# Hybrid mLSTM and convolution block on one core: other places in memory for the operands of the 512-column products

## The chip, the cores and the metric

One Trainium2 chip, one of its cores. The metric is the device time of one execution in microseconds (us); a lower one is better. In the traces PE is TensorE's matmul, PEld its weight load, DVE is VectorE, ACT is ScalarE, POOL is GpSimd and SP is SyncE, whose queue issues the DMAs.

## What is computed

One layer over 2048 tokens of 1024 channels, in float32. After an RMS norm one projection makes the inputs of an mLSTM (four heads of 256) and of a convolution module; their two outputs are concatenated and projected back:

```python
u = rmsnorm(h, norm_g[l])
proj = jnp.einsum('bsd,de->bse', u, w_in[l])          # 1024 -> 8200 columns
...
hm = mlstm_chunkwise(q, k, v, i_pre, f_pre)            # then sigmoid(o), head norm, silu(z)
...
c = glu_a * jax.nn.sigmoid(glu_g)                      # then causal conv of width 31, layernorm, silu
...
mix = jnp.concatenate([hm, c.astype(x.dtype)], axis=-1)
h = h + jnp.einsum('bse,ed->bsd', mix, w_out[l])       # 2048 -> 1024 columns
return rmsnorm(h, final_norm_g)
```

## The kernel before

Each float32 operand of the two projections is split into two float32r tiles, a high part and the rest (hi and lo). A product of two such operands is three matmuls: hi times hi, hi times lo, lo times hi, summed in PSUM.

The tokens are worked on in two halves of 1024. For a half, the normed input lies in eight tiles `u` of 128 rows by 2048 columns, hi in the first 1024 and lo in the others. The weights stream through: SyncE loads a raw piece `wr` of two blocks of 512 columns, and for each block `w_prep_` (lines 209 to 223) makes one tile `w` of 1152 columns. ACT casts the block into hi (line 221), POOL subtracts it from the block and writes lo (line 222). Four such tiles are held, and they are made up to three ahead of their use (`WAHEAD`).

`unit` (line 311) is the product loop. It has three forms:

- `fm` (line 336), for the convolution's inputs, its gate, q and k: the weight is the stationary operand (128 of its columns) and the input is the moving one (512 tokens).
- `tm2` (line 343), for v, o and z of the heads: the input is stationary (128 tokens) and the weight is moving (256 columns).
- `tm` (line 350), for v of head 0 with the gates (264 columns), and for the output projection at the end (512 columns): the input or mix tile is stationary and the weight is moving.

Every matmul has a weight load of its own, of 128 by 128. Between the products of a unit a list of mLSTM steps and of convolution taps is worked off (`ml_slot`, `pump`), so that PE's stream of 512-column products is interrupted by small products (lines 601, 627, 631, 714), while DVE runs the convolution (line 787). The output projection (1536 products) comes last; in its second half nothing else runs on PE.

Where the operands lie: the third entry of a row of the list `wsrc` is the column at which hi begins in its `w` tile; lo begins 512 columns after it (for the 528-column blocks of the 264-column products: 0 and 576):

```python
odd = wsrc[i // 2][2]
...
both = wp.tile([P, 1152], F32R, tag="w", name=f"w{i}")
o2 = 576 if n == 528 else odd + 512
hi, lo = both[:, odd : odd + n], both[:, o2 : o2 + n]
```

In the program as built, all tiles `u`, `u_m` (the mix's) and `w` begin at a byte address in their partition that is 128 modulo 256. The pieces inside `u` and `u_m` lie at multiples of 512 bytes. So the place of a stationary operand past its moving one, modulo 256 bytes, is:

| products | count | moving columns | stationary past moving |
|---|---|---|---|
| `fm`, line 336 | 3840 | 512 | 0 |
| `tm` of the output, line 350 | 1536 | 512 | 0 |
| `tm2`, line 343 | 4224 | 256 | 64 |
| `tm` of head 0, line 350 | 384 | 264 | 0 and 224, half each |

The 64 of `tm2` comes from `ODD` = 48 columns, 192 bytes, by which the moving weight is shifted.

Of the kernel before, what the change touches and what calls it, by code (L numbers as in the profile page):

```python
# [39 lines left out]
def hybrid_block_kernel(  # L40
# [15 lines left out]
    WARM = 16  # L56


    PAD, ODD = 8, 48

    def pool(name, bufs, **kw):
        return ctx.enter_context(tc.tile_pool(name=name, bufs=bufs, **kw))
# [129 lines left out]
    wsrc = []  # L192
# [714 lines left out]
    WID = {}  # L907
# [13 lines left out]
    for hf in range(2):  # L921
        s = [("g", 0)]
        for h in range(NH):
            s += [("v", h)] + ([("g", 1)] if h == 0 else []) + [("o", h), ("z", h), ("q", h), ("k", h)]
            if h < 3:
                s += [("g", 2 * h + 2), ("g", 2 * h + 3)]
        s += [("c", j) for j in range(4)]
        seq.append(s)
        for u in s:
            if u == ("v", 0):  # L930
                for _ in range(2):
                    for g in range(2):
                        wsrc.append((wv0[g], 528, 0))
            else:
                for g in range(2):
                    wsrc.append((wu[WID[u], g], 512, ODD if u[0] in "ozv" else 0))
    for b in range(4):
        for nn in range(2):
            for g in range(8):
                wsrc.append((wo[nn, g], 512, 0))  # L940

    w_load(0)
    wstate["raw"] = 1
# [183 lines left out]
```

## Time and profile before

| | |
|---|---|
| time, median of 3 runs | 2008.14 us (2007.59 to 2011.28) |
| profiled execution | 2014.07 us, span 2012.4 us |
| mean granted TensorE clock | 0.993 of full speed |
| busy: PE, PEld | 98%, 87% of the span |
| busy: DVE, ACT, POOL | 72%, 41%, 39% |
| DMA | 204.10 MB, 30.6% of 16 engines' span |

The profiled execution is one of its own: it took 2014.07 us, of which 2012.4 lie between its first and its last instruction, and is 5.9 us (0.3%) above the median of the runs. A matmul's recorded duration contains its way through the pipeline and overlaps the next one's. What a matmul costs in a row of them is therefore read from starts: the start of the first to the start of what follows, divided by their number.

### The profile page before, as it was taken

What the parts mean: (1) busy time and instruction counts of PE and PEld (TensorE: products, weight loads), DVE (VectorE), ACT (ScalarE), POOL (GpSimd) and SP (SyncE); (2) the same over time, 40 slices, a digit from 0 to 9 for tenths busy, and PEclk for the clock granted to TensorE, in tenths of its full rate; (3) what the DMA queues carried; (4) which work ended last, traced back from release to release, by engine and by line L of the source; (5) the groups of instructions that cost most, each with busy time, mean ns of one, the idle gap of its engine ahead of it and who ended that gap; (6) DMA issues with size and microseconds to landing.
All of it is one profiled execution on the core that took longest, in us unless ns stands there. A gap on an engine that the chain in (4) does not pass through costs nothing.

```text
span 2012.4 us, 29602 instructions
## 1 busy us (share of the span) xinstructions
PE 1975.9 (98%) x11562; PEld 1744.7 (87%) x11562; DVE 1445.4 (72%) x1915; ACT 827.7 (41%) x1703; POOL 792.3 (39%) x740
## 2 busy tenths in 40 slices
PE   8999999999999999999999999999999999999998
PEld 7998998899899888888889879988998887788887
DVE  6598887699679765557799998977896658733221
ACT  5233432442343246545345224424523555543332
POOL 4632432333243332433333324333432236565564
PEclk9999999999999999999999999999999999999999
DMA  4121121212122233335211211211221566766452
GB/s 151 64 69 53 58 74 43 63 49 74 42 69 74 74 110 125 113 126 162 85 53 53 69 42 59 74 53 53 64 74 53 163 220 200 248 231 231 155 190 95
DMA packets 85836, 204.10 MB, mean 101 GB/s; under 512 B 7296, under 2 KB 40256, under 8 KB 85696
## 3 DMA queue, kind: packets, MB, share of 16 engines
q1 hardware_dynamic: 85696, 202.21, 30.6%
q8 instruction: 91, 1.49, 0.3%
q14 instruction: 49, 0.40, 0.1%
HBM read 159.15 MB, written 43.03 MB: 100 GB/s over the span
## 4 chain that ended last, share of the span: by engine, by line
PE 73%; DVE 18%; DMA 3%; issue 2%; ACT 2%; POOL 0%; SPq 0%; POOLq 0%; DVEq 0%; ACTq 0%
PE gm L336 32%; PE gm L343 18%; PE gm L350 16%; DVE y L787 11%; PE num L601 3%; PE kv L601 2%; PE sk L627 1%; DMA ly<-ysc 1%; DVE sm L302 1%; DMA wr<-in_wo 1%; PE mt L714 1%; DVE ly L844 1%; DMA ysc<-y 1%; PE sk L631 1%; ACT ly L881 0%
## 5 line engine op out<-in xcount | busy, mean ns | idle before, releaser
L222 POOL TENSOR_TENSOR w<-wr,w 128x512 fp32r<-128x512 f32 (+1 forms) x392 | 603.1, 1543 | 878.2 <-ACT w L221 859.4
L336 PE MATMUL gm<-u_u,w 128*128 128x512 f32 x3840 | 908.6, 392 | 0.7 <-DVE u_u L293 0.6
L336 PEld LDWEIGHTS gm<-u_u,w 128*128 128x128 f32 x3840 | 712.5, 188 | 143.2 <-DVE u_u L293 1.3
L787 DVE SCALAR_TENSOR_TENSOR y<-c,vec,y 128x1024 f32<-128x1024 f32 x480 | 714.5, 1489 | 9.7
L343 PE MATMUL gm<-w,u_u 128*128 128x256 f32 x4224 | 521.9, 281 | 5.7 <-DVE oz L451 3.4
L343 PEld LDWEIGHTS gm<-w,u_u 128*128 128x128 f32 x4224 | 505.8, 190 | 7.6 <-DVE oz L451 3.6
L221 ACT CAST w<-wr 128x512 fp32r<-128x512 f32 (+1 forms) x392 | 241.4, 620 | 591.6 <-PE gm L336 200.2
L350 PE MATMUL gm<-w,u_m 128*128 128x512 f32 x1536 | 355.0, 392 | 3.1 <-POOL w L222 1.9
L350 PEld LDWEIGHTS gm<-w,u_m 128*128 128x128 f32 x1536 | 289.1, 189 | 64.2 <-POOL w L222 2.8
L281 DVE TENSOR_TENSOR u_m<-mr,u_m 128x1024 fp32r<-128x1024 f32 x32 | 47.2, 1475 | 77.7 <-ACT u_m L280 77.7
L1019 DVE TENSOR_TENSOR ht<-gm,ht 128x512 f32<-128x512 f32 x32 | 21.5, 687 | 112.2 <-PE gm L350 112.2
L700 POOL TENSOR_TENSOR ss<-ss,nhalf 128x1 f32<-128x1 f32 x64 | 55.5, 867 | 111.9 <-ACT sq L699 111.3
L633 DVE SCALAR_TENSOR_TENSOR w<-sk,rs,ee 128x128 f32<-128x128 f32 x64 | 22.0, 344 | 81.6 <-PE sk L631 79.1
L601 PE MATMUL kv<-v,kw 128*128 128x258 f32 x360 | 74.3, 291 | 0.6 <-DVE cs L666 0.4
L666 DVE SCALAR_TENSOR_TENSOR cs<-cs,g_so,kv 128x258 f32<-128x258 f32 x112 | 53.3, 476 | 25.1 <-PE kv L601 24.7
L639 ACT ACTIVATE kw<-sk,g_wa 128x256 fp32r<-128x256 f32 x60 | 28.3, 472 | 81.7 <-DVE w L633 81.6
L719 ACT ACTIVATE mo<-mt,vec 128x128 f32<-128x128 f32 x128 | 39.7, 362 | 52.3 <-PE mt L714 52.1
L601 PEld LDWEIGHTS kv<-v,kw 128*128 128x128 f32 x360 | 56.9, 190 | 3.2 <-DVE cs L666 0.6
L408 DVE SCALAR_TENSOR_TENSOR v<-gm,rs,v 128x256 fp32r<-128x256 f32 x64 | 29.5, 475 | 33.4 <-ACT v L407 33.4
L699 ACT ACTIVATE sq<-hm 128x257 bf16<-128x257 f32 x64 | 26.9, 420 | 64.6 <-DVE hm L694 64.4
L761 POOL TENSOR_TENSOR c<-c,g 128x512 f32<-128x512 f32 x32 | 40.9, 1284 | 30.4 <-ACT g L760 27.6
L350 PE MATMUL gm<-w,u_u 128*128 128x264 f32 x384 | 50.8, 294 | 0.0
(200 smaller groups left out, 1818.0 us busy)
## 6 DMA issues: line engine op xcount, KB each, us to landing
wr<-in_wu SPq DMA_DIRECT2D x123, 512.0 KB, 3.6
wr<-in_wo SPq DMA_DIRECT2D x64, 512.0 KB, 3.6
mr<-mixs SPq DMA_DIRECT2D x32, 512.0 KB, 4.6
ysc<-y SPq DMA_DIRECT2D x16, 512.0 KB, 2.6
mixs<-mo SPq DMA_DIRECT2D x32, 256.0 KB, 2.1
zsc<-zc SPq DMA_DIRECT2D x32, 256.0 KB, 2.1
ly<-ysc SPq DMA_DIRECT2D x16, 512.0 KB, 5.2
lz<-zsc SPq DMA_DIRECT2D x16, 512.0 KB, 6.0
```

The source lines that it names most:

```text
L221: nc.scalar.copy(hi, s)
L222: nc.gpsimd.tensor_tensor(out=lo, in0=s, in1=hi.bitcast(F32), op=ALU.subtract)
L281: nc.vector.tensor_tensor(out=l_, in0=src, in1=h_.bitcast(F32), op=ALU.subtract)
L336: nc.tensor.matmul(ps[i], wt[:, o + cb * P : o + (cb + 1) * P], at[:, tb * 512 : (tb + 1) * 512], start=st, stop=sp_,)
L343: nc.tensor.matmul(ps[i][:, t2 * 256 : (t2 + 1) * 256], at[:, t * P : (t + 1) * P], wt[:, o : o + ncol], start=st and t2 == 0, stop=sp_, s ...
L350: nc.tensor.matmul(ps[i][:, :ncol], at[:, t * P : (t + 1) * P], wt[:, o : o + ncol], start=st, stop=sp_,)
L601: nc.tensor.matmul(ps, x_, y_, start=start and i == 0, stop=stop and i == 2)
L666: nc.vector.scalar_tensor_tensor(out=cs[:, d], in0=cs[:, d], scalar=so[:, h, c : c + 1], in1=kv[:, :VW], op0=ALU.mult, op1=ALU.add,)
L700: nc.gpsimd.tensor_tensor(out=ss, in0=ss, in1=nhalf[:, 0:1], op=ALU.pow)
L719: nc.scalar.activation(mo[:, d, (cc % 2) * P : (cc % 2 + 1) * P], mt[:, d * P : (d + 1) * P], AF.Identity, scale=col(V_MG, 2 * h + d),)
L761: nc.gpsimd.tensor_tensor(out=c[:, sl], in0=c[:, sl], in1=g, op=ALU.mult)
L787: tc.keep_in_program_order(nc.vector.scalar_tensor_tensor(out=y, in0=c[:, j + i * H2 : j + (i + 1) * H2], scalar=col(V_CW, b * CW + j), in1=y,
```

## The change

It alters the third entry of `wsrc` for the weights of the 512-column products, and nothing else. The `fm` weights (stationary) are shifted by 48 columns, 192 bytes, as the `tm2` weights (moving) already were. The output weights (moving) are shifted by 16 columns, 64 bytes. In the changed program as built, the stationary operand of all 5376 products of 512 columns begins 192 bytes past the moving one, modulo 256. The places of the other products are those of before, the order of the instructions on every engine too, and a `w` tile still has room: 48 + 512 + 512 = 1072 of its 1152 columns.

```diff
-    PAD, ODD = 8, 48
+    PAD, ODD, OUT = 8, 48, 16
...
                 for g in range(2):
-                    wsrc.append((wu[WID[u], g], 512, ODD if u[0] in "ozv" else 0))
+                    wsrc.append((wu[WID[u], g], 512, ODD))
     for b in range(4):
         for nn in range(2):
             for g in range(8):
-                wsrc.append((wo[nn, g], 512, 0))
+                wsrc.append((wo[nn, g], 512, OUT))
```

## Rows read from the trace of the kernel before

**Rows 1.** The page's part 1: busy time, share of the span, instructions of each engine

```profile
span 2012.4 us, 29602 instructions
...
PE 1975.9 (98%) x11562; PEld 1744.7 (87%) x11562; DVE 1445.4 (72%) x1915; ACT 827.7 (41%) x1703; POOL 792.3 (39%) x740
```

**Rows 2.** Groups by line, shapes apart: count, busy us, mean ns, idle us before

```profile
L336 PE MATMUL gm<-u_u,w 128*128 128x512 f32 x3840 | 908.6, 392 | 0.7 <-DVE u_u L293 0.6
...
L343 PE MATMUL gm<-w,u_u 128*128 128x256 f32 x4224 | 521.9, 281 | 5.7 <-DVE oz L451 3.4 <-ACT oz L438 1.7 <-DVE v L408 0.5
...
L350 PE MATMUL gm<-w,u_m 128*128 128x512 f32 x1536 | 355.0, 392 | 3.1 <-POOL w L222 1.9 <-DVE ht L1019 1.2
```

**Rows 3.** The chain that ended last, its last long piece: start us, us

```profile
1762.31 238.51 PE gm L350 x1052
```

**Rows 4.** PE's timeline, undisturbed 512-column products: start us, us, line, count

```profile
1824.75 179.46 PE L350 MATMUL gm<-w,u_m 128*128 128x512 f32 x791
```

**Rows 5.** The same, from 307 us, and the small products after it

```profile
307.75 48.45 PE L336 MATMUL gm<-u_u,w 128*128 128x512 f32 x213
356.04 0.60 PE L627 MATMUL sk<-q,k 128*128 128x128 f32 x4
356.48 0.38 PE L631 MATMUL sk<-ident,k 128*128 128x128 f32 x2
```

**Rows 6.** The same, two runs of 256-column products and what follows each

```profile
284.73 22.94 PE L343 MATMUL gm<-w,u_u 128*128 128x256 f32 x201
307.51 17.86 PE L336 MATMUL gm<-u_u,w 128*128 128x512 f32 x78
...
469.79 13.47 PE L343 MATMUL gm<-w,u_u 128*128 128x256 f32 x113
483.10 17.18 PE L336 MATMUL gm<-u_u,w 128*128 128x512 f32 x75
```

**Rows 7.** The same, a run of 264-column products and what follows it

```profile
851.78 7.18 PE L350 MATMUL gm<-w,u_u 128*128 128x264 f32 x58
858.80 17.88 PE L336 MATMUL gm<-u_u,w 128*128 128x512 f32 x78
```

**Rows 8.** The same, 512-column products just after small ones of the mLSTM

```profile
219.69 1.08 PE L336 MATMUL gm<-u_u,w 128*128 128x512 f32 x4
220.61 0.41 PE L601 MATMUL kv<-v,kw 128*128 128x258 f32 x2
...
221.79 1.32 PE L336 MATMUL gm<-u_u,w 128*128 128x512 f32 x5
222.95 0.28 PE L601 MATMUL num<-c0h,qssl 128*128 128x258 f32 x1
```

**Rows 9.** Stretches: us, busy us of each engine, granted clock, DMA share, GB/s

```profile
495.00:583.00 88.00, 88.00 (x441) 74.64 (x440) 61.96 (x87) 32.61 (x69) 33.13 (x31) 1.00 0.17 54
...
880.00:1045.00 165.00, 157.70 (x922) 138.51 (x920) 130.37 (x165) 78.03 (x148) 54.30 (x42) 0.98 0.34 110
1045.00:1240.00 195.00, 186.46 (x1169) 167.77 (x1169) 181.74 (x238) 77.68 (x174) 70.41 (x65) 0.97 0.18 56
...
1642.00:1820.00 178.00, 172.54 (x756) 140.80 (x755) 107.32 (x85) 85.59 (x151) 105.87 (x81) 0.99 0.70 236
1820.00:2004.00 184.00, 184.00 (x813) 152.49 (x812) 46.13 (x43) 63.06 (x114) 101.17 (x93) 1.00 0.48 163
```

**Rows 10.** Stretches, products of line 336 alone: PE and PEld busy us and count

```profile
880.00:1045.00 165.00, 92.96 (x391) 71.94 (x389) 0.98 0.34 110
1045.00:1240.00 195.00, 92.59 (x384) 72.95 (x384) 0.97 0.18 56
```

**Rows 11.** Line 221 from 286 us (weights at 192 bytes), from 310 us (at 0): min/median/max ns

```profile
L221 ACT CAST w<-wr x4: 620/624/664, 286.4 to 302.3; 128x512 fp32r<-128x512 f32 x4
...
L221 ACT CAST w<-wr x8: 621/622/638, 310.2 to 345.9; 128x512 fp32r<-128x512 f32 x8
```

**Rows 12.** Line 222 in the same two stretches: min/median/max ns

```profile
L222 POOL TENSOR_TENSOR w<-wr,w x4: 1290/1493/1562, 287.2 to 303.0; 128x512 fp32r<-128x512 f32 x4
...
L222 POOL TENSOR_TENSOR w<-wr,w x8: 1291/1296/2222, 310.9 to 346.6; 128x512 fp32r<-128x512 f32 x8
```

## The prediction

> **What bounds the kernel.** I read the busy shares first: PE is busy for 98% of the span, the next engine, DVE, for 72% [rows 1]. Then the groups by line: before all 5376 products of 512 columns PE sat idle for 3.8 us in sum (0.7 and 3.1), before the 256-column ones for 5.7 us [rows 2]. So PE is not waiting for data; it works through a list, and the time is the number of products by the spacing of their starts. The chain of waits says the same where it is plainest: its last long piece is 1052 products of line 350 in 238.51 us with nothing between them, 226.7 ns each [rows 3].
>
> A duration in a group's row (392 ns) is no price, since it overlaps the next product's. The price is the spacing, which the timeline gives:
>
> - 512 columns, output: 791 products in 179.46 us. Taking off the last one's own 0.39 us, 790 spacings take 179.07 us: **226.7 ns** [rows 4].
> - 512 columns, line 336: 213 products from 307.75 to the next line's start at 356.04, 48.29 us: again 226.7 ns [rows 5].
> - 256 columns, line 343: 201 products from 284.73 to 307.51, **113.3 ns**; in another stretch 113 products from 469.79 to 483.10, **117.8 ns** [rows 6].
> - 264 columns: 58 products from 851.78 to 858.80, 121.0 ns [rows 7].
>
> In stretches of this kind the granted clock is 1.00 [rows 9], the level of 2.4 GHz. A column per period would be 213.3, 106.7 and 110.0 ns for 512, 256 and 264 columns (an estimate from the clock alone). The rest is what each product pays beyond its columns: **13.3 ns** at 512 columns, **6.7 or 11.1 ns** at 256, **11.0 ns** at 264. Each product also comes with a load of 128 by 128 that PE does beside the stream; my reading is that the rest is this load getting in the way of the moving stream's reads.
>
> What differs between these rows is the width, and the place of the stationary operand against the moving one: 0 at 512 columns, 64 at 256, 0 and 224 by turns at 264. The smallest rest is at 64. But the 256-column products show two rests at one and the same place, so the place is not all of it: there are states that last over hundreds of products.
>
> **The change, part by part.**
>
> *It adds no work.* The instructions, their order, their sizes and their waits are those of before on every engine; SP's loads and POOL's and ACT's queue keep their turn, so nothing is moved past anything.
>
> *The writes of the weight tiles* move by 192 or 64 bytes. The trace has both places: ACT's cast takes 624 ns at 192 and 622 ns at 0 [rows 11], POOL's subtraction has a minimum of 1290 and 1291 ns [rows 12]; its medians, 1493 and 1296, rest on four and eight of them. Even 200 ns more on each of the 288 tiles that move (160 for line 336, 128 for the output) would be 58 us on an engine with 1220 us free of its 2012 [rows 1], working up to three tiles ahead of PE: nothing on the path. If that cover went, the two waits for POOL before line 350, now 1.9 us in all [rows 2], would grow first.
>
> *The reads of the 5376 products* are the only term: 3840 of line 336 and 1536 of line 350 [rows 2], each with a rest of 13.3 ns now. The trace has no 512-column product at the place 192, so the new rest is bounded:
>
> - Best case, 3.3 ns: four products of line 627 take 0.44 us, 110.0 ns each for 128 columns [rows 5]. That is 106.7 plus 3.3 ns at two periods a column: their stream asks for data half as fast, and beside it the load costs almost nothing. Gain 10.0 ns by 5376, 53.8 us: 1954 us.
> - Worst case, 18.7 ns: just after the mLSTM's small products, groups of four and five 512-column products run at 230 and 232 ns (219.69 to 220.61, 221.79 to 222.95) [rows 8]. These products pay more because something in the meeting of load and stream is out of its usual step. 232.0 less 226.7, 5.3 ns by 5376, is 28.5 us more: 2037 us.
>
> I take a value nearest to the only long rows with a place other than 0, those of the 256-column products: the mean of their two rests, 8.9 ns, 4.4 ns less than now. The two rests are also the ends of this case: 6.7 ns less gives 35.8 us, 2.2 ns less gives 11.8 us. The mean gives **23.7 us**. I carry the rest in ns over, not in proportion to the columns, because there is one load per product, whatever its width.
>
> *Where a saving would not arrive.* From 1045 to 1240 us DVE is busy 181.74 of 195 us and PE already stands for 8.5; from 880 to 1045 PE stands for 7.3, and from 1642 to 1820 for 5.5 [rows 9]. There another engine or a transfer is late next. The first two hold 775 products of line 336 [rows 10], the third at most 756 of line 350. At 4.4 ns that is 6.7 us of saving, of which I write off 2 us. Elsewhere DVE has room (61.96 of 88 us in a stretch of line 336, 46.13 of 184 at the end [rows 9]), and what a faster PE triggers, DMAs first, uses half the engines at the end.
>
> **The sum.** The profiled execution's 2014.1 us (span 2012.4) becomes 2014.1 - 23.7 + 2.0 = 1992.4. The median of the runs lies 5.9 us below that execution, so the same difference against the median of 2008.1 gives **1986.4 us**, 1.1% less.
>
> The Trainium skill speaks against it: "SBUF — State Buffer", section "SBUF: two separate sides", says that PE never waits on anyone at the memory's ports and names a second, independent read port for the weight loads. By that rule operands' places could not matter, and the sum would be 2008 us.
>
> The Trainium skill ("TensorE: Matmul & The Clock Gate", section "Wait — 56ns, not 53.3ns?") gives 215.7 ns for back-to-back products of 512 columns; an estimate from it would be 11.0 ns less on each, 59 us, 1949 us. The rows here show 226.7 and never less over a long stretch.
>
> **The rivals.**
>
> *The place does not matter* (12%). The load costs a fixed 13 ns or so, because the array has to take it in, whoever reads where. For it: the 264-column products pay 11.0 ns at places 0 and 224, the 256-column ones 11.1 ns in one of their states at 64: much the same. Against it: a fixed cost could not be 6.7 ns for 201 products on end and 13.3 ns right behind them [rows 5, 6]. Time 2008 us, within 4 us. (This is also the time by the skill's rule of the two ports.)
>
> *The place is a worse one* (21%). A stationary operand 192 past the moving one is as well 64 behind it, the mirror of the 256-column products' 64 ahead. A load that starts behind the stream it runs beside may run into it for longer than one that starts at the same place, and leave it out of step for good, as rows 8 show it for a few products. It decides if the lasting spacing exceeds 226.7 ns; at 232 ns the time is 2037 us. Against it: the 264-column products, half of them at 224, 32 behind, pay 11.0 ns on the whole and thus no more than others.
>
> *The load gets wholly out of the way* (9%). Then the rest falls towards the 3.3 ns of the best case, and the time to 1954 us, or a little above it, where DVE becomes the bound between 1045 and 1240 us.
>
> *The change misses its places.* If the tiles lay elsewhere than the text of the diff suggests, anything could come out. The addresses of the program as built exclude it: all 5376 products are at 192.
>
> **How the numbers follow.** My forecast, a rest between 6.7 and 11.1 ns, has 58%, and its own range is 1972 to 1996 us. With the larger gain, faster has 67%; no change has 12%, slower 21%. About 0.2%, 4 us, is what a measurement of this kernel can tell from no change. The range begins at the best case, 1954 us, below which I leave 4%. Upward it takes in no change and half the price of the worse place, 2022 us; beyond it I leave some 14%.
>
> **What would show it.** After the change the 791 products at the end should be spaced by 220 to 224.4 ns, and the 213 of line 336 alike; the 256-column products should keep 113.3 and 117.8, and line 221 and 222 their durations. PE's idle time between 1045 and 1240 us should grow by 1 or 2 us. A spacing of 226.7 in both would prove the first rival, one of 230 or more the second. The forecast would also be wrong, with a right spacing, if the 256-column products changed their states for the worse: all of them at 117.8 instead of 113.3 would cost up to 4.5 ns by 4224, 19 us. And if lines 336 and 350 came out apart, the place modulo 256 would not be what counts, since they share it.

## The result and the profile after

| | before | after |
|---|---|---|
| median of 6 runs | 2007.89 us (2004.48 to 2011.41) | 2019.57 us (2018.53 to 2021.27) |
| profiled execution, span | 2014.07 us, 2012.4 us | 2020.03 us, 2018.3 us |
| mean granted TensorE clock | 0.993 | 0.996 |

The change makes the kernel slower by 0.56%: the ratio is 1.0056, with a 95% interval of 1.0043 to 1.0069, 11.7 us on the medians. 1986.4 us had been forecast.

A line of the page's part 1, and the groups by line with the shapes apart, answer to [rows 1] and [rows 2]:

```profile
PE 1982.8 (98%) x11562; PEld 1739.7 (86%) x11562; DVE 1442.2 (71%) x1915; ACT 828.3 (41%) x1703; POOL 794.9 (39%) x740
```

```profile
L336 PE MATMUL gm<-u_u,w 128*128 128x512 f32 x3840 | 915.9, 394 | 0.2 <-DVE oz L451 0.2
L343 PE MATMUL gm<-w,u_u 128*128 128x256 f32 x4224 | 518.7, 280 | 6.0 <-DVE oz L451 3.4 <-ACT oz L438 1.6 <-DVE v L408 0.7
L350 PE MATMUL gm<-w,u_m 128*128 128x512 f32 x1536 | 359.1, 395 | 3.0 <-POOL w L222 1.8 <-DVE ht L1019 1.2
```

Nothing new waits. PE's busy time is 6.9 us longer: line 336 has 7.3 us more, line 350 has 4.1 us more, line 343 has 3.2 us less. The spacing of the undisturbed products tells why. PE's timeline (start us, us, line, count) at the end, then from 284 us, from 469 us, and from the first 512-column product after that:

```profile
1829.64 174.58 PE L350 MATMUL gm<-w,u_m 128*128 128x512 f32 x762
```

```profile
284.79 21.47 PE L343 MATMUL gm<-w,u_u 128*128 128x256 f32 x188
306.10 6.11 PE L336 MATMUL gm<-u_u,w 128*128 128x512 f32 x26
...
307.70 47.54 PE L336 MATMUL gm<-u_u,w 128*128 128x512 f32 x207
355.08 0.60 PE L627 MATMUL sk<-q,k 128*128 128x128 f32 x4
```

```profile
469.78 12.18 PE L343 MATMUL gm<-w,u_u 128*128 128x256 f32 x102
...
481.79 50.09 PE L336 MATMUL gm<-u_u,w 128*128 128x512 f32 x214
531.72 0.61 PE L627 MATMUL sk<-q,k 128*128 128x128 f32 x4
```

Worked out as before: the output's 762 products have (174.58 - 0.39) / 761 = **228.9 ns**, against 226.7 in [rows 4]. Line 336 has two spacings now where it had one: 47.38 us / 207 = **228.9 ns** from 307.70, against 226.7 in [rows 5], and 49.93 / 214 = **233.3 ns** from 481.79. The 256-column products are as they were, 113.4 and 117.7 ns in these two stretches, as in [rows 6]. The chain's last long piece (start us, us) answers to [rows 3], 228.9 ns a product:

```profile
1765.93 240.82 PE gm L350 x1052
```

Over the whole span, waits of more than 40 ns beyond the columns left out, the starts of line 336 are 230.4 ns apart on the mean (227.7 before) and those of the output 229.0 (227.0). 2.7 ns by 3840 and 2.0 ns by 1536 make 13.4 us; line 343 gives back 0.3 ns by 4224, 1.2 us. That leaves 12.2 us, against the 11.7 us of the medians. The two profiled executions themselves lie only 5.9 us apart: the one of before is 5.9 us above its median and has some 6 us more outside these spacings. From 880 to 1045 and from 1045 to 1240 us its granted clock was 0.98 and 0.97 [rows 9]; in the changed kernel's execution it was 0.99 and 1.00.

### The profile page after: what moved, and what is told of

Read it like the earlier page. It is cut to its first block, busy times and chain, and to the rows that moved or that the text cites. A ratio compares the mean times of both kernels' runs of the same rounds, so it can differ in the third digit from the quotient of the medians.

```text
span 2018.3 us, 29602 instructions
## 1 busy us (share of the span) xinstructions
PE 1982.8 (98%) x11562; PEld 1739.7 (86%) x11562; DVE 1442.2 (71%) x1915; ACT 828.3 (41%) x1703; POOL 794.9 (39%) x740
## 4 chain that ended last, share of the span: by engine, by line
PE 78%; DVE 15%; ACT 2%; issue 2%; DMA 2%; POOL 0%; SPq 0%; POOLq 0%; DVEq 0%; ACTq 0%
PE gm L336 35%; PE gm L343 18%; PE gm L350 17%; DVE y L787 9%; PE num L601 3%; PE kv L601 2%; PE sk L627 1%; DMA ly<-ysc 1%; PE mt L714 1%; DVE ly L844 1%; PE sk L631 1%; DMA ysc<-y 1%; DVE sm L302 0%; DVE y L777 0%; DVE qssl L592 0%
## 5 line engine op out<-in xcount | busy, mean ns | idle before, releaser
L350 PE MATMUL gm<-w,u_m 128*128 128x512 f32 x1536 | 359.1, 395 | 3.0 <-POOL w L222 1.8
```

Of the source, the lines that this page charges most:

```text
L350: nc.tensor.matmul(ps[i][:, :ncol], at[:, t * P : (t + 1) * P], wt[:, o : o + ncol], start=st, stop=sp_,)
```

## The experiments

All kernels below are the one before with other shifts. `place` gives the columns by which a unit's weight tile is shifted, `OUTS` the same for the output's; a shift by n columns puts line 336's stationary operand 4n bytes past the moving one, and lines 343's and 350's 4n bytes behind it. The edits are written short, against the kernel before. Below, "place" is the stationary operand's address less the moving one's, modulo 256 bytes. Spacings in tables are means over a stretch of products at one place, without waits of over 40 ns.

**Many places in one kernel.** `s1_places`, `s2_fine`, `s3_states` and `s4_rest` give a place of its own to each q and k unit (in `s3_states` all of them have 192), to each output unit and, from the second on, to the 256-column products of each head. The edit, here in the first:

```diff
+    FM1 = {(0, 0): (64, 128), (0, 1): (64, 128), (0, 2): (32, 96), (0, 3): (160, 224),
+           (1, 0): (16, 48), (1, 1): (64, 128), (1, 2): (32, 96), (1, 3): (160, 224)}
+    def place(hf, u):
+        nm, i = u
+        if nm in "ozv":
+            return 48
+        return (FM1[hf, i][nm == "k"] if nm in "qk" else 0) // 4
+    OUTS = {(0, 0): 48, (0, 1): 32, (1, 0): 0, (1, 1): 48, (2, 0): 32, (2, 1): 16, (3, 0): 56, (3, 1): 8}
...
-                    wsrc.append((wu[WID[u], g], 512, ODD if u[0] in "ozv" else 0))
+                    wsrc.append((wu[WID[u], g], 512, place(hf, u)))
...
-                wsrc.append((wo[nn, g], 512, 0))
+                wsrc.append((wo[nn, g], 512, OUTS[b, nn]))
```

> One kernel with several places. The stationary operand's place past the moving one, modulo 256 bytes, is for the eight output units in turn 64, 128, 0, 64, 128, 192, 32, 224; for the q and k units of heads 0 to 3 of the first half 64 and 128, 64 and 128, 32 and 96, 160 and 224; of the second half 16 and 48, 64 and 128, 32 and 96, 160 and 224; g and c units at 0 as before, the 256-column products at 64 as before. Theory A (each place modulo 256 has lasting spacings of its own): units at 0 again 226.7 ns, the unit at 192 again 228.9 or 233.3 ns, and at least one of 32, 64, 96 or 128 clearly under 226.7 (220 to 224.4 at 64). Theory B (equal places are best, every shift costs): all units but those at 0 at 228 to 234 ns. Theory C (the place is not what counts, but that a tile is shifted at all, or its writes): all shifted units alike, at 228.9 or 233.3, whatever the shift.

> A second kernel with several places. The 512-column products: small shifts around 0 (stationary past moving by 4, 8 and 12 bytes, or behind it by 4, 8 and 16), further places (80, 112, 144, 176, 208), and shifts by whole 256 and 512 bytes (place 0 again). The 256-column products of one head each: 0, 0, 128, 192 in the first half, 224, 96, 160, 32 in the second, in place of 64. Theory B1 (equal places modulo 256 are best, and only they): 226.7 ns at shifts of 256 and 512 bytes, 233.3 ns at most others, already at 16 bytes. Theory D (a tile that does not begin where it did is dearer, whatever the place): 228.9 ns or more at 256 and 512 bytes too. For the 256-column products, theory B1 carried over gives their least spacing at 0 (113.3 ns or less); if 64 was their best place, all others stand at 116 to 120 ns.

> A search for a better place, with those that have not been measured. 512 columns: 20, 28, 36, 40, 44, 52, 60, 68, 76, 84, 88, 92, 104, 108, 116, 120 in the q and k units, 132, 200, 152, 212, 164, 20, 148, 88 in the output units. 256 columns: 4, 24, 112, 144 in the heads of the first half, 12, 208, 240, 252 in those of the second. Theory B1 (0 is the one good place at 512 columns, 64 at 256): none under 226.7 ns at 512 columns, none under 115.9 ns on the mean at 256. If the spacings at 512 columns scatter between 2 and 4 pieces of 6.7 ns with no rule, one or two might fall to 220 ns, and all products could then take that place for some 30 us.

One run each took 2023.53, 2023.64 and 2024.69 us (before: 2009 to 2010). The spacings in ns, a choice of some fifty places measured at 512 columns:

| place, 512 columns | 0 | 4 | 8 | 16 | 20 | 32 | 60 | 64 | 96 | 120 |
|---|---|---|---|---|---|---|---|---|---|---|
| line 336 | 226.7 | 232.3 | 230.7 | 233.3 | 233.3 | 233.2 | 230.1 | 233.3 | 234.2 | 226.7 |
| line 350 | 226.7 | | 231.7 | | 228.9 | 233.3 | | 233.3 | | 233.5 |

| place, 512 columns | 128 | 148 | 160 | 176 | 192 | 208 | 224 | 236 | 240 | 252 |
|---|---|---|---|---|---|---|---|---|---|---|
| line 336 | 232.4 | | 233.3 | 230.0 | 228.9, 233.3 | 233.3 | 233.3 | | 228.3 | 233.4 |
| line 350 | 232.4 | 228.9 | | 231.1 | 228.9 | 233.3 | 233.3 | 239.7 | 231.6 | 237.9 |

| place, 256 columns | 0 | 16 | 32 | 56 | 60 | 64 | 68 | 72 | 96 | 128 | 144 | 160 | 192 | 224 | 252 |
|---|---|---|---|---|---|---|---|---|---|---|---|---|---|---|---|
| line 343, mean | 119.7 | 117.3 | 118.4 | 120.4 | 120.0 | 115.9 | 118.1 | 120.0 | 118.1 | 118.7 | 114.7 | 119.8 | 117.6 | 116.9 | 122.8 |

No place at 512 columns lies under 226.7 ns: 0 has the least, shared by 120 at line 336 alone. Theories C and D (any shift costs, whatever the place) fall: shifts of 256 and 512 bytes, place 0 again, give 226.7, and the others differ. Theory A's forecast that 64 is good at 512 columns falls. At 256 columns the order is another one: 0 is among the worst, 64 and 144 are the best, and 4 bytes beside 64 the products stand at 118 to 120. PE's timeline of `s2_fine`, the 256-column products of a head at place 0, at the time of [rows 6]:

```profile
284.82 26.20 PE L343 MATMUL gm<-w,u_u 128*128 128x256 f32 x217
310.86 34.44 PE L336 MATMUL gm<-u_u,w 128*128 128x512 f32 x148
```

26.04 us / 217 = 120.0 ns, where the same products at 64 took 113.3. So the rest beyond the columns is 13.3 ns at place 0, at 256 columns as at 512; what 64 does to it depends on the width.

**Whole kernels at 64 and at 128, and half of the change.** In all four kernels the 256-column products stay at 64:

```diff
-                    wsrc.append((wu[WID[u], g], 512, ODD if u[0] in "ozv" else 0))
+                    wsrc.append((wu[WID[u], g], 512, ODD if u[0] in "ozv" else SHIFT))
-                wsrc.append((wo[nn, g], 512, 0))
+                wsrc.append((wo[nn, g], 512, OUT))
...
all64:    SHIFT, OUT = 16, 48
all128:   SHIFT, OUT = 32, 32
fm_only:  SHIFT, OUT = 48, 0
out_only: SHIFT, OUT = 0, 16
```

> All 5376 products of 512 columns with the stationary operand 64 bytes past the moving one, as the 256-column products have it. Theory A with 64 as a good place: spacing 220 to 224.4 ns, 12 to 36 us faster than before (1972 to 1996 us). Theory B (equal places are best): 228.9 ns or more, 12 us or more slower (2020 us or more). If 64 and 192 are mirror images of each other in cost, about 2020 us.

> All 5376 products of 512 columns with the stationary operand 128 bytes past the moving one. Theory A with pieces of memory that repeat every 256 bytes: the load is as far from the stream as it can be, spacing 216 to 224 ns, 12 to 50 us faster. If what repeats is 128 bytes, 128 is the same as 0: 226.7 ns and within 4 us of before. Theory B: 228.9 ns or more, 2020 us or more.

> Half of the change: the weights of the 3840 products of line 336 are shifted by 192 bytes, the output's 1536 products stay at place 0. If the cost is the spacing of each product (2.2 ns more in one state, 6.7 in the other), line 336 keeps its part of the loss, 8 to 12 us over the kernel before, and the output's products stand at 226.7 ns. If the loss came from the output's part, this kernel is within 4 us of the one before.

> The other half of the change: the output's 1536 products at 192, line 336's 3840 at 0. At 228.9 ns in place of 226.7, 2.2 ns by 1536: 3.4 us slower (2011 us), 228.9 ns in the last products. With the other half's loss of 9 us this makes up the change's 11.7 us. A time within 1 us of before would put the whole loss on line 336.

| kernel | median us | before us | ratio, 95% interval | line 336 / output, ns on the mean |
|---|---|---|---|---|
| all64 | 2032.56 | 2009.53 | 1.0115 (1.0099 to 1.0131) | 233.3 / 233.3 |
| all128 | 2028.50 | 2009.53 | 1.0095 (1.0081 to 1.0109) | 232.8 / 232.4 |
| fm_only | 2017.96 | 2009.53 | 1.0044 (1.0029 to 1.0059) | 230.6 / 227.0 |
| out_only | 2009.72 | 2008.58 | 1.0008 (0.9998 to 1.0017) | 227.7 / 229.0 |

The two halves of the change make 0.44% and 0.08%, together 0.52% of its 0.56%: most of the loss lies on line 336, and the output's part is too small to tell from nothing. The place at which the 256-column products are well off is the worst of the four for the 512-column ones. PE's timeline at the end of `all64` and of `out_only`:

```profile
1839.71 185.19 PE L350 MATMUL gm<-w,u_m 128*128 128x512 f32 x793
```

```profile
1829.69 171.38 PE L350 MATMUL gm<-w,u_m 128*128 128x512 f32 x748
```

By the same working 233.3 and 228.9 ns. Not all of a wider spacing arrives: in `all64` it is 5.6 ns by 3840 and 6.3 by 1536, 31 us, and 23 came. Where PE waits for others anyway a slower PE waits less: in the three stretches of [rows 9] in which it waits (from 880, 1045 and 1642 us) it stood for 21.3 us in sum, and in `all64` for 17.0. That is about half of the 8 us; the other half is not accounted for.

**Is it the place, or the address?** `abs160` moves all tiles by 32 bytes together:

```diff
-    PAD, ODD = 8, 48
+    PAD, ODD = 16, 48
```

> The kernel before with all of these tiles moved by 32 bytes together (both operands begin at 160 modulo 256 in place of 128), places past each other as before. If only the place of the one past the other counts: 226.7 ns at 512 columns, 113.3 and 117.8 ns at 256, and the time of before within 0.3%. If a place in memory by itself counts (pieces of 64 bytes, say, that an operand should begin with): 233 ns at 512 columns, and 30 us more.

2006.40 us in one run (before 2009.04), 227.0 ns in the output, 115.6 at 256 columns on the mean (115.9 before). PE's timeline at its end, 226.7 ns again:

```profile
1824.76 172.66 PE L350 MATMUL gm<-w,u_m 128*128 128x512 f32 x761
```

A common shift by 32 bytes, the only one tried, changes nothing; what counts is how the two operands stand to each other. It leaves each operand's address modulo 32 as it was, so that an effect of that is not excluded.

**Is it the width?** `widths` cuts the output's products to 448, 320, 384 and 256 columns in the four pairs of units, with the weight unshifted in the first unit of a pair and shifted by 48 columns in the second:

```diff
+                    m = ncol if st or width is None else width
                     nc.tensor.matmul(
-                        ps[i][:, :ncol], at[:, t * P : (t + 1) * P], wt[:, o : o + ncol],
+                        ps[i][:, :m], at[:, t * P : (t + 1) * P], wt[:, o : o + m],
```

> The output's products cut in width, all but the first of each sum: 448 columns in the first two output units, 320, 384 and 256 in the next pairs, at place 0 in the first unit of a pair and 64 in the second; same stationary tile, same moving tile, one product per bank. The columns left out are not summed, so the output is not the reference's and the time not to be compared. If the width of the product turns the order of the places round (why 256 columns stand better at 64 and 512 at 0): at 256 columns about 120 ns at place 0 and 113.3 or 117.8 at 64, at 384 and 448 the reverse. If it is the kind of unit (two products in a bank, the other operand shifted, the mLSTM beside it) that made the 256-column products prefer 64: place 0 is better at all widths, by 6.7 ns.

With 256 columns the weights came too slowly, so that PE worked in short groups. PE's timeline inside one group at place 0 and inside one at 64:

```profile
1900.25 4.84 PE L351 MATMUL gm<-w,u_m 128*128 128x256 f32 x39
...
1918.52 2.66 PE L351 MATMUL gm<-w,u_m 128*128 128x256 f32 x22
```

Taking off the last one's own 0.28 us, 4.56 / 38 = 120.0 ns at place 0 and 2.38 / 21 = 113.3 ns at 64; other groups at 64 have 117 to 119. So the same unit, with the same tiles, one product per bank and no mLSTM beside it, prefers 64 at 256 columns, and 0 at 512 (226.7 and 233.3 ns, before and `all64`). It is the width. Between the two the order does not turn just once: in the longest runs, at 320 columns place 0 has 146.9 ns and 64 has 146.8, at 384 place 0 has 174.0 (173.3 once settled, the columns, 160, and 13.3) and 64 has 174.7, and at 448 place 0 has 202.6, in one stretch 206, and 64 has 202.3. The reverse that was expected at 384 and 448 came at 384 alone, and small.

**Why 228.9 in one stretch and 233.3 in another?** `s3_states` puts the q and k units at 192 and the 256-column products before them at places from 16 to 80; it took 2029.24 us in one run (before 2007.53).

> Two questions. First, the 256-column products near their place 64: the stationary operand past the moving one by 48, 80, 56, 72 in the heads of the first half, 60, 68, 52, 16 in the second. If 64 is the middle of a good region, some of them stand at 113.3 ns throughout, which all units could be given (up to 10 us to win); if only 64 itself is good, all lie at 116 to 120 ns. Second, the q and k units at place 192, the other 512-column products of line 336 at 0. In the trace of the change 233.3 ns followed wherever the 256-column products just before stood at 117.8, and 228.9 ns where they stood at 113.3 (eight of eight heads). Theory E (a state carried from one product to the next): with other places before them, q and k show again just 228.9 or 233.3 and each for the whole run up to the first small products. Theory F (something at those times, a transfer or another engine, sets it): the heads keep the spacings they had, 228.9 in heads 0 and 1 of the first half and head 1 of the second, 233.3 in the rest. The output units take eight more places (24, 100, 184, 56, 244, 236, 72, 176): theory B1 expects none under 226.7 ns.

PE's timeline in the first head and in the third, inside the q and k units:

```profile
134.76 39.60 PE L336 MATMUL gm<-u_u,w 128*128 128x512 f32 x169
```

```profile
491.64 38.62 PE L336 MATMUL gm<-u_u,w 128*128 128x512 f32 x168
```

39.21 / 168 = 233.4 ns and 38.23 / 167 = 228.9 ns: the other way round than in the changed kernel. Six other heads have 228.9 (one of them 229.3, disturbed), so two states and no third, held over all of q and k. Their time within the kernel (theory F) does not set them. What fits is that the products before leave something behind: in the changed kernel and in `fm_only` 233.3 follows 117.8 and 228.9 follows 113.3 in every head, and the two heads where the traces of these kernels differ (at about 945 and 1140 us) differ in both spacings. In `s3_states`, where q and k stand as in the changed kernel and other products do not, six of the eight heads have the other of the two spacings. What is carried over stays open. The search at places near 64 found none that is good throughout.

**What 64 is worth at 256 columns.** `tm2_0` puts those products at 0, with `ODD = 0`.

> The 4224 products of 256 columns at place 0 in place of 64, the 512-column ones at 0 as before. From the sweep (119.75 ns at 0, against 115.9 at 64) 3.9 ns by 4224 is 16 us: about 2025 us. If the sweep's spacings were an effect of the mixture of places in one kernel, within 4 us of before.

2021.73 us against 2007.53, ratio 1.0066 (1.0050 to 1.0082), and 119.7 ns on the mean: 3.8 ns by 4224 is 16 us, 14 came.

**Other good places.** `tm2_144` shifts the 256-column products by 28 columns; `all120` shifts line 336's weights by 30 and the output's by 34.

> The kernel before with the 4224 products of 256 columns at place 144 in place of 64; the 512-column products at 0. In the search head 3 of the first half had 114.75 ns there, against 115.72 ns in the same head at 64. If that holds in all heads, about 1 ns by 4224, 4 us faster (2004 us), at the edge of what can be told. If it was the state that this head came in, within 4 us of before, either way.

> All 5376 products of 512 columns with the stationary operand 120 bytes past the moving one: the only other place of the search with 226.7 ns over an undisturbed unit of 96 products. If 0 and 120 are equal, within 4 us of before, and 226.7 ns in the last 791 products. If 226.7 ns at 120 is one of several states there, others show up (229 to 233 ns), and the time is 5 to 30 us longer. A gain would need states under 226.7 ns, of which the search showed none.

`tm2_144`: 2005.63 us against 2007.96, ratio 0.9986 (0.9977 to 0.9995), 114.7 ns on the mean over all heads, so it was the place. `all120`: 2005.91, ratio 0.9987 (0.9978 to 0.9995). Its two lines come apart, though both stand at 120. PE's timeline in line 336 and in the output:

```profile
309.76 40.51 PE L336 MATMUL gm<-u_u,w 128*128 128x512 f32 x178
...
1809.61 186.59 PE L350 MATMUL gm<-w,u_m 128*128 128x512 f32 x799
```

226.7 ns and 233.3 ns. That the time is nevertheless no longer has two reasons in the trace. Line 336 is at 227.4 on its mean, 0.3 under place 0. And in the first half of the output PE has no room to lose: from 1642 to 1820 us it stood for 5.5 us before [rows 9], and stands for 0.2 now (the stretch's columns as there):

```profile
1642.00:1820.00 178.00, 177.79 (x771) 144.88 (x770) 100.58 (x87) 89.03 (x157) 94.66 (x88) 1.00 0.68 233
```

These two make 6.5 us. The output's 6.5 ns by 1536 are 10 us more, and the time is 2 us less, so 12 us want a reason; where the other half went is not shown.

`s5_512` asks whether the lines differ because what counts is the place modulo 512, with q and k at 120 and 376 or 20 and 276 by turns:

> Why line 336 has 226.7 ns at place 120 and line 350 233.5 at the same place modulo 256: modulo 512 line 336's stood at 120 and line 350's at 376. Here q and k units take 120 and 376 by turns in the first half, 20 and 276 in the second; the output units 120, 376, 120, 376, 120, 376, 20, 276. Theory G (the place counts modulo 512): 226.7 ns at 120 and 233.5 at 376 in both lines; at 20 and 276, where line 336 had 233.3 at 20 and line 350 228.9 at 276, the same exchange. Theory H (only modulo 256 counts, and the lines differ by their kind or the state they start in): 120 and 376 alike within each line, about 227 in line 336 and 233.5 in line 350.

Line 336 has 226.8 ns at 120 and at 376, line 350 has 233.6 and 233.5; at 20 and 276 line 336 has 233.2 and 233.3, line 350 has 228.9 at both. So it is not the place modulo 512 that sets the lines apart. (The kernel took 2010.57 us in one run.) They agree at the six places measured in both that are multiples of 32 bytes (0, 32, 64, 128, 192, 224), but for line 336's second spacing at 192, and come apart at 8, 20, 88, 120, 176, 240 and 252 (208 agrees). At line 336 the stationary tile is the shifted one, at line 350 the moving one, so off the multiples of 32 bytes each operand's own address modulo 32 differs between the lines too. Whether that is the reason was not tried.

**The good places together.** `best`: line 336 at 120, the output at 0, the 256-column products at 144.

```diff
-                    wsrc.append((wu[WID[u], g], 512, ODD if u[0] in "ozv" else 0))
+                    wsrc.append((wu[WID[u], g], 512, 28 if u[0] in "ozv" else 30))
```

> The good places together: line 336's products at 120, the output's at 0, the 256-column ones at 144. By spacings: line 336 227.4 ns, the output 227.0, the 256-column products 114.7 against 115.9. The 256-column part was measured at 0.14% under the kernel before; the kernel with all 512-column products at 120 at 0.13% under it, although its output products stood at 233.5 ns, 6.5 ns by 1536 or 10 us more. If gains add up, 2 and 12 us: 1994 us, 0.7% faster. If the 10 us had not arrived at the end anyway, 2003 us.

**1999.93 us** (1998.25 to 2001.35) against 2008.58, ratio 0.9958 (0.9944 to 0.9973): 0.42% faster than the kernel before, and so faster than the changed one too. PE's timeline in line 343, in line 336 and in the output:

```profile
279.73 25.21 PE L343 MATMUL gm<-w,u_u 128*128 128x256 f32 x221
304.77 1.54 PE L336 MATMUL gm<-u_u,w 128*128 128x512 f32 x6
...
309.78 40.51 PE L336 MATMUL gm<-u_u,w 128*128 128x512 f32 x178
...
1819.78 169.48 PE L350 MATMUL gm<-w,u_m 128*128 128x512 f32 x747
```

113.3, 226.7 and 226.7 ns. The spacings give 1.2 ns by 4224 and 0.3 by 3840, 6 us; 8.6 came, within the interval (5.4 to 11.2 us).

## Why the prediction was wrong

**What held.** PE is the bound and the time is products by spacing: against the 11.7 us stand 13.4 us of wider spacing at the 512-column products, less 1.2 us. The change added nothing else: the weight casts take 619 ns on the mean (619 before), POOL's subtractions 1551 (1541), and POOL keeps PE waiting for 1.8 us. No engine took PE's place. That the place matters held too: 226.7 to 239.7 ns by place alone. The Trainium skill's rule ("SBUF — State Buffer", "SBUF: two separate sides") that PE never waits at the memory's ports would have all places alike; the measurement decides against it here, or against reading it as a rule for PE's two own reads.

**The step that failed** is: "I take a value nearest to the only long rows with a place other than 0, those of the 256-column products: the mean of their two rests". It took the small rest at 64 for an effect of being off 0, and carried it over to another width and to another place. Both failed. At 256 columns 0 is a bad place and 64 a good one (120.0 and 113.3 to 117.8 ns); at 512 it is the reverse (226.7 and 233.3), and the output's unit shows both orders, by its width alone (`widths`, `all64`). At 192, the change's place, 512 columns pay 15.6 or 20.0 ns in place of 13.3.

The rows of before held a warning that was read too lightly: the 264-column products, half of them at 0 and half at 224, paid 11.0 ns all the same (121.2 and 121.3 ns at the two places, on the mean), which does not fit a place that is good or bad by itself. And every 512-column product stood at one place, so that nothing in the trace could price another. Of the two rests that came, 15.6 ns lies within the bounds of 3.3 to 18.7, and 20.0 beyond the worse of them.

**The rivals.** "The place is a worse one" came true in kind, at a lower price: 232 ns was taken from products just after interruptions [rows 8], and on the mean line 336 stands at 230.4, the output at 229.0. The picture behind it, a load that runs behind the stream, is not shown: 240, 16 behind, costs 1.6 ns at line 336 and 224 costs 6.6. "The place does not matter" is refuted, and "the load gets wholly out of the way" was met at no place. The time lies inside the range, at its upper end, but the sign was wrong.

**What would show it.** The test "lines 336 and 350 apart" was right to be there: at 192 both have 228.9 ns, but line 336 has 233.3 besides, and at 120 they are apart, so the place modulo 256 is not the whole quantity.

## What to carry to other kernels

The spacing of back-to-back float32r matmuls, each with its own weight load, depends on how the stationary operand lies to the moving one modulo 256 bytes, by up to 13 ns on 227, and off the multiples of 32 bytes not in the same way for two kinds of product; a few columns of spare room in a tile are enough to choose. The best place must be measured for each width and each kind of product, in one kernel that gives every unit a place of its own, since the best places at 256 columns (64 and 144) cost 233.3 ns at 512 (144 measured at line 336 alone), and the best at 512 (0) is a bad one at 256. And price a wider or narrower spacing only where PE does not wait: where it waits for others, part of it does not arrive.

## What was not expected of the hardware

Some of the lasting rests come in steps. With 2.4 GHz, 16 periods are 6.67 ns; 226.7, 233.3, 113.3 and 120.0 ns are the columns and 2, 3, 1 and 2 such steps. 228.9 and 117.8 are 7/3 and 5/3 of a step, and single starts in the changed kernel's output show how: 226, 229 and 232 ns, again and again, 7 steps in three products. Others (230.0 and 232.4 ns) are no whole thirds of a step.

Which of two patterns runs is a state that outlives a change of width and of line: 233.3 ns follows 117.8, and 228.9 follows 113.3, in all heads of two traces, until the first small products end it.

A place can be as narrow as one column: 256-column products have 115.9 ns on the mean at 64, and 120.0 at 60.
